# A two-layer decoder trunk on one core: FFN activations transposed by VectorE and a pass through DRAM, and a start by single k tiles over two DMA queues

## The chip, the cores and the metric

The kernel runs on one core of a Trainium2 chip. The metric is device time in microseconds from one launch. Three runs of the kernel before gave 1171.79, 1172.56 and 1173.34 us; the median is 1172.56 us.

The engines are called by their names in the profile: PE (TensorE, matrix products), PEld (its weight loads), DVE (VectorE), ACT (ScalarE), POOL (GpSimd), and SP (SyncE), which here only issues DMAs. SPq and ACTq are the DMA-issuing rows of SP and ACT.

## What is computed

A trunk of two layers over 256 tokens of width 1024. Each layer is a half-step SwiGLU FFN, a gated mix of three token mixers (a diagonal state-space model, sparse attention, forgetting attention), and another half-step FFN; a final RMSNorm follows. The change is in the four FFNs and in the start of the first one:

```python
def swiglu(h, w_gate, w_up, w_down):
    return (jax.nn.silu(h @ w_gate) * (h @ w_up)) @ w_down

x = x + 0.5 * swiglu(rms_norm(x, g), w_gate, w_up, w_down)   # hidden width 2816 = 22 k tiles of 128
```

## The kernel before, in words

**Split products.** Every weight is loaded as fp32 in a *unit* of two k tiles (256 rows) by up to 512 columns: `raw`, 512 KB, four buffers. ACT rounds it to fp32r (`hi<-raw`), DVE takes the rest (`lo<-raw,hi`). The tokens' side is split in the same way: `h0h`, `h0l` (k tiles 0 to 3 of the FFN's input), `h1h`, `h1l` (4 to 7), and `ath`, `atl` (the hidden activations). Each k tile and half of the tokens then takes three matmuls: high by high, high by low, low by high (`mm_tok`).

**An FFN.** `ffn` goes through the 2816 hidden columns in five chunks of 512 and one of 256. A chunk has four units of the gate weights and four of the up weights, so 96 matmuls into four PSUM banks (`ps_acc`). Halfway ACT computes `s` (SiLU of the gate part, line 662); at the end DVE computes `act = up * rstd * s` (line 670), with tokens on the partitions. The down product contracts over the hidden columns, so it needs `act` with hidden columns on the partitions. The generator `up_T` (lines 627 to 640) makes it: per pair of k tiles four PE transposes of 128x128 into a scratch PSUM bank `ps_t`, one ACT copy to `ath`, one DVE subtraction to `atl`. That is 176 transposes in 44 groups of four for the whole program. The down product (lines 677 to 683) then runs over 22 k tiles, twice (two halves of 512 output columns).

**What sets the order.** The program writes one instruction stream per engine in a fixed order; at run time each engine goes through its stream in order and waits on semaphores. While the stream is written, a `Clock` adds up estimated costs per engine. After each group of matmuls `tick` (line 325) lets background generators such as `up_T` go one step if their input should be ready by that clock, and `feed` issues the `hi` and `lo` work of the units ahead: up to four and three units ahead of PE. A unit's DMA is issued on SP when its buffer is free, that is behind the `lo` of the unit four before it (line 378). `prep_once`, `prep_bias` and `prep_layer` are background generators too; they compute constants of the mixers, most of them on DVE, beside the first FFN of each layer.

**The start.** `run` (line 1395) issues the column constants `cols`, then on the one queue SP in turn pieces of the transposed input `xT` (by 1, 1, 2 and 4 k tiles) and gate units; the first two units have one k tile each. `first_T` makes `h0h`/`h0l` of a k tile from `xT`. `loads` (line 1223) then brings the input `x` with tokens on the partitions, from which ACT computes the sums of squares for `rstd`; `s` of the first chunk waits for it.

Of the kernel before, what the change touches and what calls it, by code (L numbers as in the profile page):

```python
# [18 lines left out]
P = 128  # L19
# [33 lines left out]


# [23 lines left out]
def plan(a):  # L78
# [3 lines left out]
    def add(w, k0, nk, c0, n):  # L82
        k = k0
        while k < k0 + nk:
            m = min(2 if len(units) > 1 else 1, k0 + nk - k)
            units.append((w[k * P:(k + m) * P, c0:c0 + n].rearrange("(k p) c -> p k c", p=P), m, n))
            k += m

    def ffn(l, which):
        wg, wu, wd = (a[f"{which}_w_{n}"][l] for n in ("gate", "up", "down"))  # L90
        for i, (c0, n) in enumerate(f_chunks()):
            order = [(wg, 0), (wu, 0), (wg, 4), (wu, 4)] if i == 0 else [(wg, 0), (wg, 4), (wu, 0), (wu, 4)]
            for w, k0 in order:
                add(w, k0, 4, c0, n)
        for d in range(2):
            for k0 in range(0, FK, 4):
                add(wd, k0, min(4, FK - k0), d * 512, 512)
# [136 lines left out]
class Trunk:  # L234
# [112 lines left out]
    def feed_dma(self, upto):  # L347
        while self.n_dma < min(upto, len(self.units)):
            ap, nk, n = self.units[self.n_dma]
            t = self.rawp.tile([P, 2, 512], F32, tag="raw", name="raw")  # L350
            self.clock.after("dma", self.freed.get(self.n_dma - RAW_BUFS, 0.0))
            self.nc.sync.dma_start(t[:, :nk, :n], ap)
            self.raw[self.n_dma] = t
            self.n_dma += 1

    def feed_hi(self, upto):
        while self.n_hi < min(upto, len(self.units)):
            i = self.n_hi
            _, nk, n = self.units[i]
            self.feed_dma(i + 1)  # L360
            hi = self.piecep.tile([P, 2, 512], F32R, tag="hi", name="hi", bufs=HI_AHEAD + 1)
            self.nc.scalar.activation(hi[:, :nk, :n], self.raw[i][:, :nk, :n], AF.Copy)
            self.split_tiles[i] = hi
            self.n_hi += 1

    def feed_lo(self, upto):
        nc = self.nc
        while self.n_lo < min(upto, len(self.units)):
# [5 lines left out]
            nc.vector.tensor_tensor(lo[:, :nk, :n], src, hi[:, :nk, :n].bitcast(F32), op=OP.subtract)  # L374
# [25 lines left out]
    def mm_tok(self, ps, xs, k0, nk, n, first, last):  # L400

        mm = self.nc.tensor.matmul
        for k, hi, lo in self.weights(nk, n):
            k += k0
            xh, xl = xs(k)
            for t in range(2):
                c = slice(t * P, t * P + P)
                mm(ps[t][:, :n], xh[:, c], hi, start=k == first, stop=False)
# [207 lines left out]
    def ffn(self, nxt):  # L616
# [4 lines left out]
        with tc.tile_pool(name="ffn", bufs=1, side="left") as pool:  # L621
# [3 lines left out]
            pend = None  # L625

            def up_T(act, k0, nk):
                yield act
                for b in range(0, nk, 2):
                    i, ps = yield from self.bank()  # L630
                    for j in range(2):
                        for t in range(2):
                            nc.tensor.transpose(ps[:, j * T + t * P:j * T + t * P + P],
                                                act[:, t, (b + j) * P:(b + j + 1) * P], self.ident)
                    yield ps
                    h, lw = ath[:, k0 + b:k0 + b + 2], atl[:, k0 + b:k0 + b + 2]
                    p3 = ps.rearrange("p (k t) -> p k t", k=2)
                    nc.scalar.activation(h, p3, AF.Copy)
                    nc.vector.tensor_tensor(lw, p3, h.bitcast(F32), op=OP.subtract)
                    self.tfree(i)  # L640

            for ci, (c0, n) in enumerate(f_chunks()):
# [17 lines left out]
                act = pool.tile([P, 2, 512], F32, tag="act", name="act", bufs=2)  # L660
# [8 lines left out]
                for t in range(2):  # L669
                    nc.vector.scalar_tensor_tensor(act[:, t, :n], pu[t][:, :n], rstd[:, t:t + 1], s[:, t, :n],  # L670
                                                   op0=OP.mult, op1=OP.mult)
                if pend:
                    self.finish(pend)
                pend = self.spawn(up_T(act, c0 // P, n // P), -1)
            ax = lambda k: (ath[:, k], atl[:, k])
            gens = []
            for d in range(2):
                ps = self.acc()
                last = nxt is None and d == 1
                for k0 in range(0, FK - LAST if last else FK, 2):  # L680
                    if d == 0 and k0 + 2 > FK - 2:
                        self.finish(pend)
                    self.mm_tok(ps, ax, k0, 2, 512, 0, FK - 1)
# [557 lines left out]
    def prep_bias(self, pool, begun):  # L1241
# [20 lines left out]
        yield from self.units_on(6)  # L1262
# [118 lines left out]
    def first_T(self, xT, k):  # L1381

        hi, lo = (n[:, k % 4] for n in self.nexthT[k // 4])
        g = self.cols[:, C_FFN1 + k:C_FFN1 + k + 1]
# [10 lines left out]
    def run(self):  # L1395
# [8 lines left out]
        warm = cst.tile([P, 1], F32, name="warm")  # L1404
        nc.scalar.activation(warm, self.ones[:, 0:1], AF.Silu)
# [5 lines left out]
        for l in range(L):  # L1411
            with tc.tile_pool(name="prep", bufs=1, side="right") as pp:
                gens = []
                if l == 0:
                    xT = pp.tile([P, KT, T], F32, tag="xT", name="xT")
                    for k, n, w in ((0, 1, 1), (1, 1, 2), (2, 2, 4), (4, 4, 4)):
                        nc.sync.dma_start(xT[:, k:k + n], a["l_xT"][:, k:k + n])
                        self.feed_dma(w)
                    self.nexthT = [self.new_hT(ch) for ch in range(2)]
                    for k in range(KT):  # L1420
                        self.first_T(xT, k)
                        if k < 4:
                            self.feed_lo(min(k + 1, LO_AHEAD))
                    begun = lambda: self.n_used > 7
                    self.s_gens = [self.spawn(self.loads(self.ss, lambda: self.n_used > 3, begun), -1)]
# [81 lines left out]
```

## Time and profile before

| | |
|---|---|
| median of three runs | 1172.56 us |
| profiled execution, its own time | 1173.79 us |
| its span, first to last instruction | 1172.0 us |
| PE busy | 1157.6 us (99%) |
| PEld, DVE, ACT, POOL busy | 83%, 67%, 52%, 7% |
| DMA | 208.07 MB, mean 178 GB/s |

The profiled execution lasted 1.79 us longer than its span, and 1.23 us longer than the median. A group row reads: line, engine, operation, output<-inputs, shapes, count, then busy us and mean ns of one, then idle time of that engine just before and who ended it. Line 217 is the helper through which every engine instruction is recorded, so groups are told apart by their tiles. Matmuls overlap in the pipe: one of 512 columns is shown with 0.39 us, but the next starts 0.227 us after it. So the cost of a PE instruction is read from the starts of its neighbours.

### The profile page before, as it was taken

What the parts mean: (1) busy time and instruction counts of PE and PEld (TensorE: products, weight loads), DVE (VectorE), ACT (ScalarE), POOL (GpSimd) and SP (SyncE); (2) the same over time, 40 slices, a digit from 0 to 9 for tenths busy, and PEclk for the clock granted to TensorE, in tenths of its full rate; (3) what the DMA queues carried; (4) which work ended last, traced back from release to release, by engine and by line L of the source; (5) the groups of instructions that cost most, each with busy time, mean ns of one, the idle gap of its engine ahead of it and who ended that gap; (6) DMA issues with size and microseconds to landing.
All of it is one profiled execution on the core that took longest, in us unless ns stands there. A gap on an engine that the chain in (4) does not pass through costs nothing.

```text
span 1172.0 us, 16482 instructions
## 1 busy us (share of the span) xinstructions
PE 1157.6 (99%) x5990; PEld 973.8 (83%) x5990; DVE 784.0 (67%) x1380; ACT 608.2 (52%) x905; POOL 85.7 (7%) x135
## 2 busy tenths in 40 slices
PE   8999999999999999999999999999999999999997
PEld 6888888998787888888888888889987788888885
DVE  4876975798777665555578646558977776555554
ACT  5544454644765554444455545446548655444442
POOL 1000700000210700000000000000013000000000
PEclk9999999999999999999999999999999999999999
DMA  7656655466444666646566546544744456655661
GB/s 270 223 173 178 209 162 178 153 189 183 124 149 152 193 198 190 184 146 223 193 189 181 174 143 221 185 150 146 234 128 140 157 189 197 190 179 162 206 193 69
DMA packets 115554, 208.07 MB, mean 178 GB/s; under 512 B 7486, under 2 KB 27376, under 8 KB 115472
## 3 DMA queue, kind: packets, MB, share of 16 engines
q1 hardware_dynamic: 114000, 203.51, 55.5%
q0 software_dynamic: 1184, 3.11, 1.0%
q8 instruction: 47, 0.77, 0.3%
q10 hardware_dynamic: 288, 0.39, 0.1%
q14 instruction: 35, 0.29, 0.1%
HBM read 205.91 MB, written 1.07 MB: 177 GB/s over the span
## 4 chain that ended last, share of the span: by engine, by line
PE 96%; ACT 2%; DVE 1%; DMA 1%; issue 0%; SPq 0%; ACTq 0%; DVEq 0%
PE ps_acc L217 88%; PE ps_t L217 8%; DMA raw<-in_ffn_w_gate_dram 1%; ACT vT L217 1%; ACT hi L217 0%; ACT st L217 0%; DVE lo L217 0%; SPq L217 0%; DVE st L217 0%; ACT ahl L217 0%; DVE rsqt L217 0%; DVE bl L217 0%; DVE rstd L217 0%; ACT bh L217 0%; ACT junk L217 0%
## 5 line engine op out<-in xcount | busy, mean ns | idle before, releaser
L217 DVE TENSOR_TENSOR lo<-raw,hi 128x1024 fp32r<-128x1024 f32 (+3 forms) x415 | 468.5, 1136 | 228.7 <-PE ps_acc L217 190.2
L217 ACT ACTIVATE hi<-raw 128x1024 fp32r<-128x1024 f32 (+3 forms) x415 | 408.3, 989 | 356.2 <-PE ps_acc L217 278.2
L217 PE MATMUL ps_acc<-hi,h0h 128*128 128x512 f32 (+3 forms) x544 | 212.1, 390 | 2.7 <-ACT hi L217 2.6
L217 PE MATMUL ps_acc<-hi,h1h 128*128 128x512 f32 (+3 forms) x544 | 208.4, 383 | 0.0
L217 PE MATMUL ps_acc<-lo,h0h 128*128 128x512 f32 (+3 forms) x544 | 205.6, 378 | 1.0 <-DVE lo L217 1.0
L217 PE MATMUL ps_acc<-hi,h0l 128*128 128x512 f32 (+3 forms) x544 | 205.2, 377 | 0.0
L217 PE MATMUL ps_acc<-hi,h1l 128*128 128x512 f32 (+3 forms) x544 | 204.3, 376 | 0.0
L217 PE MATMUL ps_acc<-lo,h1h 128*128 128x512 f32 (+3 forms) x544 | 204.2, 375 | 0.0
L217 PE MATMUL ps_acc<-hi,ath 128*128 128x512 f32 x352 | 139.0, 395 | 0.0
L217 PE MATMUL ps_acc<-hi,atl 128*128 128x512 f32 x352 | 137.3, 390 | 0.0
L217 PE MATMUL ps_acc<-lo,ath 128*128 128x512 f32 x352 | 137.2, 390 | 0.0
L217 PEld LDWEIGHTS ps_acc<-hi,h0h 128*128 128x128 f32 x544 | 103.0, 189 | 20.9 <-ACT hi L217 3.9
L217 PEld LDWEIGHTS ps_acc<-lo,h0h 128*128 128x128 f32 x544 | 103.2, 190 | 18.4 <-DVE lo L217 2.3
L217 PEld LDWEIGHTS ps_acc<-hi,h1h 128*128 128x128 f32 x544 | 102.6, 189 | 19.1 <-issue 1.8
L217 PEld LDWEIGHTS ps_acc<-hi,h0l 128*128 128x128 f32 x544 | 103.0, 189 | 18.1
L217 PEld LDWEIGHTS ps_acc<-hi,h1l 128*128 128x128 f32 x544 | 102.5, 188 | 18.0
L217 PEld LDWEIGHTS ps_acc<-lo,h1h 128*128 128x128 f32 x544 | 102.6, 189 | 16.8 <-issue 0.2
L217 PEld LDWEIGHTS ps_acc<-hi,atl 128*128 128x128 f32 x352 | 66.1, 188 | 13.8
L217 PEld LDWEIGHTS ps_acc<-hi,ath 128*128 128x128 f32 x352 | 66.2, 188 | 13.5 <-issue 0.4
L217 PEld LDWEIGHTS ps_acc<-lo,ath 128*128 128x128 f32 x352 | 66.2, 188 | 13.3 <-issue 0.2
L217 DVE TENSOR_TENSOR atl<-ps_t,ath 128x512 fp32r<-128x512 f32 x44 | 30.4, 691 | 28.9 <-ACT ath L217 28.7
L217 ACT ACTIVATE ath<-ps_t 128x512 fp32r<-128x512 f32 x44 | 26.1, 594 | 32.4 <-PE ps_t L217 32.4
(270 smaller groups left out, 1227.8 us busy)
## 6 DMA issues: line engine op xcount, KB each, us to landing
raw<-in_ffn_w_down_dram SPq DMA_DIRECT2D x88, 512.0 KB, 4.3
raw<-in_ffn_w_up_dram SPq DMA_DIRECT2D x80, 512.0 KB, 4.1
raw<-in_ffn_w_gate_dram SPq DMA_DIRECT2D x79, 512.0 KB, 4.3
raw<-in_w_in_dram SPq DMA_DIRECT2D x56, 512.0 KB, 4.6
raw<-in_w_out_dram SPq DMA_DIRECT2D x16, 512.0 KB, 3.7
raw<-in_ffn_w_gate_dram SPq DMA_DIRECT2D x18, 256.0 KB, 2.8
raw<-in_ffn_w_up_dram SPq DMA_DIRECT2D x16, 256.0 KB, 2.8
raw<-in_w_in_dram SPq DMA_DIRECT2D x16, 256.0 KB, 2.8
```

The source lines that it names most:

```text
L217: return f(*args, **kw)
```

## The change

`up_T` no longer uses PE. DVE writes `act` with its columns reordered: hidden column 16i+m of a chunk goes to place 32m+i (in the chunk of 256: 8i+m), so successive results are written 128 bytes apart. DVE then transposes `act` by blocks of 32x32 within each group of 32 partitions (`STREAM_TRANSPOSE at<-act`, one instruction per half of the tokens). SP writes `at` to a scratch tensor in DRAM (`actd<-at`, 512 KB in 256 runs of 2 KB for a chunk of 512) and, once that has landed, reads it back (`aT<-actd`, 512 KB in 1024 runs of 512 bytes) so that hidden column 4p+k of the chunk stands on partition p. `ath` and `atl` are computed from `aT` in SBUF instead of from PSUM. The rows of `w_down` are loaded in the same order ("(p k) c"). `act` has one buffer instead of two, and the down product waits chunk by chunk (`ups`) while the stream is written.

At the start, `xT` is issued from ACT's queue ahead of its table load, and the gate units from SP's; the first two units have two k tiles each but are loaded and split by single k tiles, alternating with `first_T`; for these k tiles the two matmuls that need `lo` come last. `x` is called for earlier (`n_used > 1`), and the bias rows later (10 units instead of 6).

```diff
--- before.py
+++ after.py
@@ plan @@
-    def add(w, k0, nk, c0, n):
+    def add(w, k0, nk, c0, n, rows="(k p) c -> p k c"):
         k = k0
+        part = w[k0 * P:(k0 + nk) * P, c0:c0 + n].rearrange(rows, p=P)
         while k < k0 + nk:
-            m = min(2 if len(units) > 1 else 1, k0 + nk - k)
-            units.append((w[k * P:(k + m) * P, c0:c0 + n].rearrange("(k p) c -> p k c", p=P), m, n))
+            m = min(2, k0 + nk - k)
+            units.append((part[:, k - k0:k - k0 + m], m, n))
...
-                add(wd, k0, min(4, FK - k0), d * 512, 512)
+                add(wd, k0, min(4, FK - k0), d * 512, 512, "(p k) c -> p k c")
@@ feed_dma, feed_hi, feed_lo (SINGLE = 2) @@
-            self.nc.sync.dma_start(t[:, :nk, :n], ap)
+            for j in self.parts(self.n_dma):
+                self.nc.sync.dma_start(t[:, j, :n], ap[:, j])
...
+    def parts(self, i):
+        nk = self.units[i][1]
+        return [slice(j, j + 1) for j in range(nk)] if i < SINGLE else [slice(0, nk)]
...
-            self.nc.scalar.activation(hi[:, :nk, :n], self.raw[i][:, :nk, :n], AF.Copy)
+            if i >= SINGLE:
+                self.nc.scalar.activation(hi[:, :nk, :n], self.raw[i][:, :nk, :n], AF.Copy)
...
-            nc.vector.tensor_tensor(lo[:, :nk, :n], src, hi[:, :nk, :n].bitcast(F32), op=OP.subtract)
+            for j in self.parts(i):
+                if i < SINGLE:
+                    self.first_T(j.start + 2 * i)
+                    nc.scalar.activation(hi[:, j, :n], src[:, j], AF.Copy)
+                nc.vector.tensor_tensor(lo[:, j, :n], src[:, j], hi[:, j, :n].bitcast(F32), op=OP.subtract)
@@ mm_tok @@
+            early = self.n_used <= SINGLE
+            if early:
+                for t in range(2):
+                    c = slice(t * P, t * P + P)
+                    mm(ps[t][:, :n], xh[:, c], hi, start=k == first, stop=False)
+                    mm(ps[t][:, :n], xl[:, c], hi, start=False, stop=False)
             for t in range(2):
                 c = slice(t * P, t * P + P)
+                if early:
+                    mm(ps[t][:, :n], xh[:, c], lo, start=False, stop=k == last)
+                    continue
...
@@ ffn @@
-            pend = None
+            ups = []
 
             def up_T(act, k0, nk):
+                n, m = nk * P, nk * 32
                 yield act
+                at = pool.tile([P, 2, 512], F32, tag="at", name="at")
+                for t in range(2):
+                    nc.vector.transpose(at[:, t, :n], act[:, t, :n])
+                    yield
+                yield at
+                scr = self.dram.tile([2, P, 512], F32, name="actd")
+                nc.sync.dma_start(bass.AP(tensor=scr.tensor, offset=scr.offset, ap=[[n, P], [P * n, 2], [1, n]]), at[:, :, :n])
+                yield scr
+                aT = pool.tile([P, 8, P], F32, tag="aT", name="aT")
+                nc.sync.dma_start(aT[:, :, :m], bass.AP(tensor=scr.tensor, offset=scr.offset, ap=[[m, P], [32 * n, 8], [1, m]]))
+                yield aT
                 for b in range(0, nk, 2):
-                    i, ps = yield from self.bank()
-                    for j in range(2):
-                        for t in range(2):
-                            nc.tensor.transpose(ps[:, j * T + t * P:j * T + t * P + P],
-                                                act[:, t, (b + j) * P:(b + j + 1) * P], self.ident)
-                    yield ps
-                    h, lw = ath[:, k0 + b:k0 + b + 2], atl[:, k0 + b:k0 + b + 2]
-                    p3 = ps.rearrange("p (k t) -> p k t", k=2)
-                    nc.scalar.activation(h, p3, AF.Copy)
-                    nc.vector.tensor_tensor(lw, p3, h.bitcast(F32), op=OP.subtract)
-                    self.tfree(i)
+                    h, lw = (x[:, k0 + b:k0 + b + 2].rearrange("p k (a j) -> p k a j", a=8) for x in (ath, atl))
+                    a4 = aT[:, :, b * 32:b * 32 + HD].rearrange("p a (k j) -> p k a j", k=2)
+                    nc.scalar.activation(h, a4, AF.Copy)
+                    nc.vector.tensor_tensor(lw, a4, h.bitcast(F32), op=OP.subtract)
+                    yield
...
-                act = pool.tile([P, 2, 512], F32, tag="act", name="act", bufs=2)
+                act = pool.tile([P, 2, 512], F32, tag="act", name="act")
...
-                    nc.vector.scalar_tensor_tensor(act[:, t, :n], pu[t][:, :n], rstd[:, t:t + 1], s[:, t, :n],
-                                                   op0=OP.mult, op1=OP.mult)
-                if pend:
-                    self.finish(pend)
-                pend = self.spawn(up_T(act, c0 // P, n // P), -1)
+                    o, p, g = (x.rearrange(f"p {r} -> p i m", i=32) for x, r in
+                               ((act[:, t, :n], "(m i)"), (pu[t][:, :n], "(i m)"), (s[:, t, :n], "(i m)")))
+                    nc.vector.scalar_tensor_tensor(o, p, rstd[:, t:t + 1], g, op0=OP.mult, op1=OP.mult)
+                ups.append(self.spawn(up_T(act, c0 // P, n // P), -1))
...
-                    if d == 0 and k0 + 2 > FK - 2:
-                        self.finish(pend)
+                    if d == 0 and k0 % 4 == 0:
+                        self.finish(ups[k0 // 4])
@@ prep_bias @@
-        yield from self.units_on(6)
+        yield from self.units_on(10)
@@ run @@
-        warm = cst.tile([P, 1], F32, name="warm")
-        nc.scalar.activation(warm, self.ones[:, 0:1], AF.Silu)
...
-                    for k, n, w in ((0, 1, 1), (1, 1, 2), (2, 2, 4), (4, 4, 4)):
-                        nc.sync.dma_start(xT[:, k:k + n], a["l_xT"][:, k:k + n])
-                        self.feed_dma(w)
+                    for k, n in ((0, 1), (1, 1), (2, 2), (4, 4)):
+                        nc.scalar.dma_start(xT[:, k:k + n], a["l_xT"][:, k:k + n])
+                    warm = cst.tile([P, 1], F32, name="warm")
+                    nc.scalar.activation(warm, self.ones[:, 0:1], AF.Silu)
+                    self.feed_dma(RAW_BUFS)
                     self.nexthT = [self.new_hT(ch) for ch in range(2)]
-                    for k in range(KT):
-                        self.first_T(xT, k)
-                        if k < 4:
-                            self.feed_lo(min(k + 1, LO_AHEAD))
+                    self.xT = xT
+                    self.feed_lo(SINGLE)
+                    for k in range(4, KT):
+                        self.first_T(k)
...
-                    self.s_gens = [self.spawn(self.loads(self.ss, lambda: self.n_used > 3, begun), -1)]
+                    self.s_gens = [self.spawn(self.loads(self.ss, lambda: self.n_used > 1, begun), -1)]
```

SP, the very start of the program, before: pieces of `xT` and units of weights in turn.

```order
L217 DMA cols<-in_l_cols_dram 128x114
L217 DMA xT<-in_l_xT_dram 128x256
L217 DMA raw<-in_ffn_w_gate_dram 128x512
L217 DMA xT<-in_l_xT_dram 128x256
L217 DMA raw<-in_ffn_w_gate_dram 128x512
L217 DMA xT<-in_l_xT_dram 128x512
L217 DMA raw<-in_ffn_w_gate_dram 128x2x512
L217 DMA raw<-in_ffn_w_up_dram 128x2x512
L217 DMA xT<-in_l_xT_dram 128x1024
L217 DMA raw<-in_ffn_w_up_dram 128x2x512
```

The same place on SP now:

```order
L221 DMA cols<-in_l_cols_dram 128x114
L221 DMA raw<-in_ffn_w_gate_dram 128x512 x4
L221 DMA raw<-in_ffn_w_up_dram 128x2x512 x2
L221 DMA raw<-in_ffn_w_gate_dram 128x2x512 x2
L221 DMA raw<-in_ffn_w_up_dram 128x2x512 x2
L221 DMA x<-in_x_dram 128x1024 x2
```

The four pieces of `xT` have left SP; they are the first four rows of ACT's stream, ahead of its table load. Four single k tiles of gate weights stand directly behind `cols`.

DVE, a chunk of 512 hidden columns in the second FFN of layer 0, before: `act`, then `atl` one unit later.

```order
L217 TENSOR_TENSOR lo<-raw,hi 128x1024 x3
L217 SCALAR_TENSOR_TENSOR act<-ps_acc,rstd,s 128x512 x2
L217 TENSOR_TENSOR lo<-raw,hi 128x1024
L217 TENSOR_TENSOR atl<-ps_t,ath 128x512 x2
L217 TENSOR_TENSOR lo<-raw,hi 128x1024 x7
```

The same place on DVE now:

```order
L221 TENSOR_TENSOR lo<-raw,hi 128x1024 x3
L221 SCALAR_TENSOR_TENSOR act<-ps_acc,rstd,s 128x32x16 x2
L221 TENSOR_TENSOR lo<-raw,hi 128x1024
L221 STREAM_TRANSPOSE at<-act 128x512 x2
L221 TENSOR_TENSOR lo<-raw,hi 128x1024 x5
L221 TENSOR_TENSOR atl<-aT,ath 128x512 x2
L221 TENSOR_TENSOR lo<-raw,hi 128x1024 x2
```

Two instructions per chunk are new, and `atl` has moved back by five units.

SP, the end of the same FFN, before (from the last up units of 512 columns on):

```order
L217 DMA raw<-in_ffn_w_up_dram 128x2x512 x4
L217 DMA raw<-in_ffn_w_gate_dram 128x2x256 x4
L217 DMA raw<-in_ffn_w_up_dram 128x2x256 x4
L217 DMA raw<-in_ffn_w_down_dram 128x2x512 x22
L217 DMA raw<-in_ffn_w_gate_dram 128x2x512 x2
```

The same place now:

```order
L221 DMA raw<-in_ffn_w_gate_dram 128x2x256
L221 DMA actd<-at 128x2x512
L221 DMA raw<-in_ffn_w_gate_dram 128x2x256 x2
L221 DMA aT<-actd 128x8x128
L221 DMA raw<-in_ffn_w_gate_dram 128x2x256
L221 DMA raw<-in_ffn_w_up_dram 128x2x256 x4
L221 DMA raw<-in_ffn_w_down_dram 128x2x512 x2
L221 DMA actd<-at 128x2x512
L221 DMA raw<-in_ffn_w_down_dram 128x2x512 x4
L221 DMA aT<-actd 128x8x128
L221 DMA raw<-in_ffn_w_down_dram 128x2x512 x2
L221 DMA actd<-at 128x2x256
```

Each trip stands as a write, two to four units of weights, and a read, on the queue that loads the weights; the last read (`aT<-actd 128x8x64`) stands behind the tenth down unit of 22.

## Rows read from the trace of the kernel before

**Rows 1.** Page, part 1, busy time of each engine, and part 4, the chain.

```profile
PE 1157.6 (99%) x5990; PEld 973.8 (83%) x5990; DVE 784.0 (67%) x1380; ACT 608.2 (52%) x905; POOL 85.7 (7%) x135
...
PE 96%; ACT 2%; DVE 1%; DMA 1%; issue 0%; SPq 0%; ACTq 0%; DVEq 0%
```

**Rows 2.** Who waited for whom, PE: total us, times, longest.

```profile
PE ps_acc L217 <- ACT hi L217: 2.6, 1, 2.6
```

**Rows 3.** Groups by line and shape, PE: the transposes of act.

```profile
L217 PE MATMUL ps_t<-ident,act 128*128 128x128 f32 x176 | 26.6, 273 | 0.0
```

**Rows 4.** The chain in order of time: start us, us, what.

```profile
38.68 21.13 PE ps_acc L217 x93
59.82 0.44 PE ps_t L217 x4
```

**Rows 5.** Timeline of PE around one group: start us, us, instruction.

```profile
59.42 0.39 PE L217 MATMUL ps_acc<-hi,h0l 128*128 128x512 f32 x1
59.66 0.60 PE L217 MATMUL ps_t<-ident,act 128*128 128x128 f32 x4
60.01 0.47 PE L217 MATMUL ps_acc<-hi,h0h 128*128 128x512 f32 x1
60.32 0.39 PE L217 MATMUL ps_acc<-lo,h0h 128*128 128x512 f32 x1
```

**Rows 6.** Groups by line and shape, DVE.

```profile
L217 DVE TENSOR_TENSOR lo<-raw,hi 128x1024 fp32r<-128x1024 f32 x333 | 405.4, 1223 | 189.3 <-PE ps_acc L217 156.8 <-ACT hi L217 22.5 <-issue 8.1
...
L217 DVE TENSOR_TENSOR atl<-ps_t,ath 128x512 fp32r<-128x512 f32 x44 | 30.4, 691 | 28.9 <-ACT ath L217 28.7
...
L217 DVE TENSOR_TENSOR_SCAN w<-mg,w 128x256 f32<-128x256 f32 x8 | 5.1, 674 | 0.0
```

**Rows 7.** Instructions on the tile act, 40 to 110 us: ns min/median/max, starts.

```profile
L217 DVE SCALAR_TENSOR_TENSOR act<-ps_acc,rstd,s x6: 750/751/752, 56.5 to 102.5; 128x512 f32<-128x512 f32 x6
```

**Rows 8.** Stretches: us, busy (count) of PE, PEld, DVE, ACT, POOL, clock, DMA share, GB/s.

```profile
117.20:146.50 29.30, 29.30 (x175) 24.57 (x174) 26.57 (x42) 14.51 (x22) 21.76 (x42) 1.00 0.64 209
429.10:451.80 22.70, 22.70 (x105) 18.84 (x105) 12.46 (x13) 10.85 (x12) 0.00 (x0) 1.00 0.62 186
```

**Rows 9.** Timeline of SP's DMA issues in one chunk.

```profile
62.81 2.54 SPq L217 DMA_DIRECT2D raw<-in_ffn_w_gate_dram  x2
```

**Rows 10.** DMA queues (packets, MB, share), then issues (count, KB each, us to landing).

```profile
q1 hardware_dynamic: 114000, 203.51, 55.5%
...
raw<-in_ffn_w_up_dram SPq DMA_DIRECT2D x80, 512.0 KB, 4.1
...
raw<-in_ffn_w_up_dram SPq DMA_DIRECT2D x16, 256.0 KB, 2.8
...
out_dram<-y_t SPq DMA_DIRECT2D x2, 320.0 KB, 2.7
```

**Rows 11.** Timeline of the first 24 us: SP, ACT and PE.

```profile
3.53 0.43 SPq L217 DMA_DIRECT2D raw<-in_ffn_w_gate_dram  x1
...
3.85 0.51 ACT L217 ACTIVATE h0h<-xT,cols 128x256 fp32r<-128x256 f32 x1 [1.62 <-DMA xT<-in_l_xT_dram]
...
4.59 0.63 ACT L217 ACTIVATE hi<-raw 128x512 fp32r<-128x512 f32 x1 [0.23 <-DMA raw<-in_ffn_w_gate_dram]
...
11.40 1.06 ACT L217 ACTIVATE hi<-raw 128x1024 fp32r<-128x1024 f32 x1 [0.85 <-DMA raw<-in_ffn_w_gate_dram]
...
14.04 1.70 ACT L217 ACTIVATE h1h<-xT,cols 128x256 fp32r<-128x256 f32 x4 [1.18 <-DMA xT<-in_l_xT_dram]
...
23.34 0.39 PE L217 MATMUL ps_acc<-hi,h1h 128*128 128x512 f32 x1
```

**Rows 12.** The same view, stretches of the start.

```profile
5.30:10.00 4.70, 4.29 (x12) 2.38 (x12) 1.82 (x3) 1.15 (x2) 0.34 (x1) 1.00 0.91 315
10.00:12.50 2.50, 0.00 (x0) 0.00 (x0) 0.49 (x2) 1.60 (x3) 0.00 (x0) 1.00 1.03 402
12.50:17.00 4.50, 3.73 (x9) 2.80 (x10) 3.57 (x7) 3.32 (x7) 0.00 (x0) 0.62 0.70 232
```

More of the change, by code (lines that the diff above doesn't have):

```diff
@@ L52 @@
 WARM = 9
+SINGLE = 2
 RAW_BUFS = 4
@@ L1378, in prep_layer, with first_T @@
             yield
-    def first_T(self, xT, k):
+    def first_T(self, k):
         hi, lo = (n[:, k % 4] for n in self.nexthT[k // 4])
-        g = self.cols[:, C_FFN1 + k:C_FFN1 + k + 1]
+        g, xT = self.cols[:, C_FFN1 + k:C_FFN1 + k + 1], self.xT
         self.nc.scalar.activation(hi, xT[:, k], AF.Copy, scale=g)
```

## The prediction

> **What bounds the kernel now.** I read the page first: PE is busy 99% of the span and carries 96% of the chain that ended last [rows 1]. So only what shortens PE's stream, or the time in which it stands, can move the end. Then who waited for whom: the longest wait of PE on another engine is 2.6 us, once, for the first two-tile unit [rows 2]. The change touches both: it takes instructions out of PE's stream, and it rebuilds the start.
>
> **The transposes leave PE.** 176 of them stand in PE's stream [rows 3], in 44 groups of four. Their busy time (26.6 us) is not their price, since they overlap in the pipe. The price is read from starts: 93 matmuls of a chunk take 21.13 us, 0.227 each [rows 4]. Without the group, the matmul that starts at 60.32 would have started two steps after 59.42, at 59.87; it is 0.45 us late, of which 0.35 is the group and the rest the slower first matmul behind it [rows 5]. The chain gives the same 0.44 to a group [rows 4]. Gain: 44 x 0.445 = 19.6 us. Nothing takes their place on PE, and nothing else runs beside them, so all of it is on the path, if `ath`, `atl`, `hi` and `lo` still come in time.
>
> **What DVE gets.** 48 block transposes (40 of 512 columns, 8 of 256), and 48 `act` writes with a stride. The trace shows neither. For a transpose of 128x512 the nearest row is `atl`, same shape and type, 0.69 us; 512 columns more make `lo` 0.53 longer, which leaves out any fixed part, and the slowest rate, a scan of 256 columns in 0.67, makes it 1.35 [rows 6]. `act` costs 0.75 now [rows 7]; at the scan's rate 1.35. I take 0.69 and an unchanged 0.75, so +1.4 us a chunk (bounds +1.1 to +3.9). In the second FFN a chunk has 12.46 us of DVE work in 22.70 [rows 8]; with 1.4 more that is 13.9 in 21.8, and at the upper bound 16.4. The tight place is the end of the first FFN, where the mixers' constants are computed too: 26.57 busy of 29.30 [rows 8]. There three groups leave PE (28.0 stay) and the transposes of one long and the short chunk come, 1.4 + 0.8, giving 28.8. The 0.8 of excess lies within the one unit (2.7 us of PE) that `lo` is ahead, and the constants may slide into the down product. I price it at nothing; at the upper bounds (3.9 + 2.0) DVE would be 4.5 us behind. `atl` and `ath` keep their number and shape, and read SBUF instead of PSUM.
>
> [...]
>
> **The way through DRAM.** Each of 24 chunks adds a write and a read on SP's queue, 48 DMAs, and the read waits for the write. Behind the waiting read stand weight units, for which ACT's `hi` waits, and then PE. How much cover is there? The first gate unit of a chunk is issued at 62.81 [rows 9], and PE takes it when the chunk before ends, one period after the `act` at 56.5, at 79.2 [rows 4, 7]. Of these 16.4 us the landing takes about 4.1 [rows 10], `hi` 1.06 [rows 11] and `lo` 1.22 [rows 6]; 10 us are left. Two more units stand between write and read, 5.4 us of PE. So a write has to take over 15 us before PE sees it. A store of 320 KB to DRAM took 2.7 us, a load of 512 KB 4.1 [rows 10]. I expect 3 to 5 us for the write and 4 to 7 for the read, and no wait of PE. For the last chunk the read stands behind the tenth down unit and its tiles are needed with the eleventh; 16.4 us ahead are six units, so even there about 16 us remain.
>
> The 16 DMA engines are busy 62% of a chunk, 14.1 us [rows 8]. The write, 256 runs of 2 KB, is like a unit: at the queue's mean (55.5% of 16 x 1172 us over 114000 packets, 91 ns) 16 packets per engine, 1.5 us [rows 10]. The read has 64 packets of 512 bytes per engine: 5.8 us at 91 ns. But units with the same 256 packets at half the bytes land in 2.8 instead of 4.1 us [rows 10], so a packet costs largely by its bytes, and I take 41 ns, 2.6 us. Sum 18.2 of 21.8 us (21.4 at 91 ns). It fits either way.
>
> **The start.** Before, 48 matmuls lie between PE's first and the first that uses `h1h`, at 23.34 [rows 11]; at 0.227 they would need 10.9 us. [...] The two-tile gate unit, issued at 3.53, lands at 11.4; the second half of `xT` at 14.0 [rows 11]. The issue at 3.53 is SP's seventh, in steps of about 0.47; the fourth gate tile is now its fifth, at 2.6, 0.9 earlier, and `xT`'s second half, SP's ninth before, is ACT's fourth, 2.4 earlier. If landings move by as much, the tile is there at 10.5 and all of `xT` by 11.6. Then ACT does `h1h` (1.7, to 13.3), `hi` of the first up unit (1.06), DVE its `lo` (1.22, to 15.6), and 24 matmuls are left, 5.4: 21.0 instead of 23.34. Gain 2.3 us. Floor, if no transfer is late: ACT was ready at 2.2 (3.85 less its wait of 1.62 [rows 11]) and is so four issues of 0.43 later, at 3.9; it does four times 0.51 + 0.63 [rows 11], then the same chain: 17.9, a gain of 5.4. Other end: no earlier landing and, with waits at each tile, a lower clock for longer: 24.0, a loss of 0.7. I take 2.3, nearest to the row of the landing. `x` is asked for one unit earlier, so `s` should still free its banks in time.
>
> Sum for the profiled execution: 1173.79 - 19.6 - 2.3 = 1151.9; it lay 1.23 above the median of the runs, so 1150.7.
>
> **Rivals.**
> 1. The start gives nothing. For it: from 10.0 to 12.5 the DMA engines are at 100% of their share and 402 GB/s [rows 12], so two queues load the same engines, and `xT`'s last 512 KB now shares them with the gate tiles instead of standing behind. Against: from 5.3 to 10.0 only 315 GB/s moved. Price: T = 1150.7 + 2.3 + up to 0.7, about 1153.4. [...]
> 2. The start reaches its floor: 3.1 us more, 1147.6. It needs landings that the trace does not show.
> 3. DVE is late in the first FFN: the new operations run at the upper bounds, and PE waits for `lo` in the last chunks, 2 to 4.5 us: 1154.7, to 1155.2. If the third and fourth chunk are late too, 1157. For it: DVE is 91% busy there [rows 8]; against: the rows of two inputs at 0.69 to 0.75 for 512 columns. [...]
> 4. Slower than before: the DMA engines become the bound by the read in 512-byte runs. A chunk now takes 22.70; with 14.1 + 1.5 of other transfers it takes longer when 64 packets exceed 7.1 us, 112 ns each. At 120 ns it is 23.24, +0.54 on each of 20 long chunks and some 1 us on the short ones, less 2.3: 1182. Against: that is more than the mean of packets 3.5 times as large.
>
> **How the numbers follow.** Forecast 0.55, rival 1 0.17, rival 2 0.10, rival 3 0.11, rival 4 0.07, of which 0.02 end near its point of balance. The forecast's own range follows from the start's bounds, 1148 to 1154; with rivals 1 to 3 it becomes 1146.5 to 1157, which leaves out rival 4 and a little beyond. About 0.2% (2.3 us) is what a measurement of this kernel can tell from no change. Faster by more: all but rival 4, 0.93; within it 0.02; slower 0.05.
>
> **What would show it.** No `ps_t<-ident,act` on PE, and a chunk's chain of 96 matmuls in 21.8 us instead of 22.7; if chunks take longer, name who PE waits for: `lo` means rival 3, `hi` behind `raw` means rival 4. `STREAM_TRANSPOSE` near 0.7 us and `act` near 0.75. `actd` landing under 15 us. The first `h1h` matmul near 21.0, with the clock no lower than before. The prediction is wrong if PE's waits after the start exceed a few us in sum, or if the start ends later than 24.

## The result and the profile after

The changed kernel takes 1155.93 us (median of 4 runs, 1154.11 to 1158.91) beside 1172.95 of the kernel before in the same comparison: ratio 0.9854, 95% interval 0.9842 to 0.9866, so 17.1 us less (15.7 to 18.5). The forecast was 1150.7, 21.9 less. Of the expected gain 4.8 us are missing. The time lies in the stated range of 1146.5 to 1157, but not in the forecast's own part of it, 1148 to 1154. The profiled execution of the changed kernel is the slowest of its four (1158.91, 3.0 above the median), which has to be kept in mind wherever its microseconds are summed.

The page of the changed kernel, busy time of the engines and the chain that ended last:

```profile
PE 1139.4 (98%) x5814; PEld 956.4 (83%) x5814; DVE 819.0 (71%) x1427; ACT 606.5 (52%) x908; POOL 87.5 (8%) x135
...
PE 85%; DMA 6%; DVE 5%; ACT 2%; issue 1%; SPq 0%; DVEq 0%; ACTq 0%
```

PE has 176 instructions fewer, as many as there were transposes [rows 1, 3]. But PE's share of the chain fell from 96 to 85%, and DMA and DVE stand there with 11: the end now hangs on something else in places. The groups that belong to the four FFNs' activations, over the whole program (busy us, mean ns of one, idle before), DVE's and then ACT's:

```profile
L221 DVE SCALAR_TENSOR_TENSOR act<-ps_acc,rstd,s 128x512 f32<-128x512 f32 x40 | 43.1, 1164 | 9.4 <-PE ps_acc L221 9.4
...
L221 DVE TENSOR_TENSOR atl<-aT,ath 128x512 fp32r<-128x512 f32 x44 | 29.0, 697 | 62.0 <-ACT ath L221 62.0
L221 DVE STREAM_TRANSPOSE at<-act 128x512 f32<-128x512 f32 x40 | 25.7, 682 | 0.0
```
```profile
L221 ACT ACTIVATE ath<-aT 128x512 fp32r<-128x512 f32 x44 | 25.6, 625 | 47.7 <-DMA aT<-actd 47.7
```

The transpose costs 682 ns (0.69 us was taken). `act` went from 751 ns [rows 7] to 1164. And DVE stands 62.0 us ahead of `atl`, where it stood 28.9 before [rows 6]: the wait for the trip through DRAM is inside DVE's line, by way of ACT. The landings (issues, KB each, median us from issue to landing; the down weights took 4.3 before):

```profile
raw<-in_ffn_w_down_dram SPq DMA_DIRECT2D x88, 512.0 KB, 5.2
...
actd<-at SPq DMA_DIRECT2D x20, 512.0 KB, 5.8
aT<-actd SPq DMA_DIRECT2D x20, 512.0 KB, 5.5
```

The start: timeline of ACT and PE, then the view by windows, whose stretches answer to [rows 12].

```profile
10.92 1.70 ACT L221 ACTIVATE h1h<-xT,cols 128x256 fp32r<-128x256 f32 x4
...
20.20 0.39 PE L221 MATMUL ps_acc<-hi,h1h 128*128 128x512 f32 x1
```
```profile
5.30:10.00 4.70, 3.68 (x10) 2.93 (x11) 2.30 (x5) 2.85 (x6) 0.34 (x1) 1.00 1.03 391
10.00:12.50 2.50, 2.50 (x13) 2.06 (x12) 2.41 (x6) 2.36 (x6) 0.00 (x0) 1.00 1.04 374
12.50:17.00 4.50, 3.62 (x15) 2.48 (x14) 4.23 (x6) 3.69 (x5) 0.00 (x0) 1.00 0.68 194
```

`h1h` begins 3.1 us earlier and without a wait. PE works from 10.0 to 12.5, where it stood, and the granted clock stays at its upper level after that (1.00 from 10.0 to 24.0). The 1.00 of the first stretch has to be read with care: the record of the granted clock begins at 9.4, and the matmuls from 6.9 to 8.2 start 0.43 us apart, the pace that the kernel before shows from 14.4 to 16.5 at the lower level, a granted clock of 0.50. The first `h1h` matmul is at 20.20 instead of 23.34 [rows 11], and a chunk of the second FFN takes 21.76 us on PE instead of 22.69.

**Where the gain is lost.** PE runs the same 5088 accumulating matmuls (those into `ps_acc`) in both kernels, from the 25th on in the same order, so the same one can be looked up in both traces. The 801st stands in the second half of the first layer's first down product, behind all 11 groups of that FFN; before, then after, in the timeline of PE:

```profile
196.23 0.39 PE L217 MATMUL ps_acc<-hi,atl 128*128 128x512 f32 x1
```
```profile
194.21 0.39 PE L221 MATMUL ps_acc<-hi,atl 128*128 128x512 f32 x1
```

It is 2.0 us earlier. It should be 3.1 (start) and 11 groups by 0.445 (4.9) earlier, 8.0. So 6.0 us are lost by then. At the 3301st (761.11, and 751.42) 8.1 are lost, at the last matmul 7.9: the rest of the program keeps its gain, but for 2.1 us in the second layer's first FFN, which e7 (below), with the same order on every engine, does not show. The place is that first down product, up to the turn from its first half to its second. Its stretches after (us, busy of PE, PEld, DVE, ACT, POOL, clock, DMA share, GB/s), and one of the kernel before:

```profile
125.00:141.00 16.00, 16.00 (x94) 14.20 (x93) 10.19 (x15) 8.52 (x13) 9.07 (x26) 1.00 1.01 336
141.00:155.00 14.00, 14.00 (x58) 10.45 (x56) 13.43 (x16) 7.70 (x9) 13.61 (x15) 1.00 0.64 207
155.00:171.00 16.00, 12.38 (x56) 9.26 (x55) 14.98 (x19) 5.53 (x10) 1.55 (x2) 0.96 0.55 170
```
```profile
146.00:170.00 24.00, 24.00 (x142) 19.64 (x141) 16.20 (x25) 12.67 (x20) 1.14 (x2) 1.00 0.43 144
```

Before, DVE has 7.8 us of air in 24, once the constants are done. After, it first stands for 5.8 of 16 us, most of it in the 4.13 us ahead of one `atl`, and then works 28.4 of 30 while PE stands for 3.6. Its timeline shows why (start us, us; idle before and its cause in brackets), and PE's what came of it:

```profile
135.96 1.23 DVE L221 TENSOR_TENSOR lo<-raw,hi 128x1024 fp32r<-128x1024 f32 x1 [0.38 <-PE ps_acc L221]
141.32 1.39 DVE L221 TENSOR_TENSOR atl<-aT,ath 128x512 fp32r<-128x512 f32 x2 [4.13 <-ACT ath L221]
...
167.01 0.69 DVE L221 TENSOR_TENSOR bp<-pm,pm 64x512 f32<-64x512 f32 x1
167.73 1.22 DVE L221 TENSOR_TENSOR lo<-raw,hi 128x1024 fp32r<-128x1024 f32 x1
168.87 1.28 DVE L221 SCALAR_TENSOR_TENSOR x<-ps_acc,x 128x512 f32<-128x512 f32 x2
```
```profile
166.93 0.39 PE L221 MATMUL ps_acc<-hi,atl 128*128 128x512 f32 x1
169.61 0.33 PE L221 MATMUL ps_t<-ident,x 128*128 128x128 f32 x1 [2.29 <-DVE x L221]
```
```profile
169.60:173.40 3.80, 3.52 (x13) 2.89 (x13) 2.33 (x4) 3.21 (x8) 0.00 (x0) 0.55 0.60 190
```

The last line is a stretch of the view by windows. Who PE waited for between 20 and 190 us (total, times, longest):

```profile
PE ps_t L221 <- DVE x L221: 2.6, 2, 2.3
PE ps_acc L221 <- DVE lo L221: 0.9, 1, 0.9
```

`x`, which PE transposes for the next norm, stands behind DVE's backlog: `bp`, the last piece of the mixers' constants, and a `lo` come right ahead of it. PE waits 0.9 for a `lo` and 2.6 for `x`, and after the long wait the granted clock is 0.55 for 3.8 us, and 0.50 from 169.9 to 173.2, where matmuls of 512 columns start 0.43 us apart instead of 0.23; that costs an estimated 0.45 x 3.8 = 1.7. The sum is 5.2 of the 6.0; the rest is not assigned. PE's own order has a part in it too: the transposes of `x` stand behind the 714th accumulating matmul, where they stood behind the 717th, and three matmuls are 0.7 us.

### The profile page after: what moved, and what is told of

Read it like the earlier page. It is cut to its first block, busy times and chain, and to the rows that moved or that the text cites. A ratio compares the mean times of both kernels' runs of the same rounds, so it can differ in the third digit from the quotient of the medians.

```text
span 1157.1 us, 16231 instructions
## 1 busy us (share of the span) xinstructions
PE 1139.4 (98%) x5814; PEld 956.4 (83%) x5814; DVE 819.0 (71%) x1427; ACT 606.5 (52%) x908; POOL 87.5 (8%) x135
## 4 chain that ended last, share of the span: by engine, by line
PE 85%; DMA 6%; DVE 5%; ACT 2%; issue 1%; SPq 0%; DVEq 0%; ACTq 0%
PE ps_acc L221 79%; PE ps_t L221 6%; DVE lo L221 2%; DMA aT<-actd 2%; DMA actd<-at 2%; DMA raw<-in_ffn_w_down_dram 1%; ACT hi L221 1%; DMA raw<-in_ffn_w_gate_dram 1%; DVE pm L221 0%; DVE atl L221 0%; DVE act L221 0%; DVE vT L221 0%; DMA raw<-in_ffn_w_up_dram 0%; ACT vT L221 0%; DMA xT<-in_l_xT_dram 0%
## 5 line engine op out<-in xcount | busy, mean ns | idle before, releaser
L221 ACT ACTIVATE hi<-raw 128x1024 fp32r<-128x1024 f32 (+4 forms) x416 | 407.2, 986 | 344.6 <-PE ps_acc L221 205.3
L221 DVE TENSOR_TENSOR lo<-raw,hi 128x1024 fp32r<-128x1024 f32 (+4 forms) x416 | 465.6, 1132 | 159.4 <-PE ps_acc L221 89.8
L221 PE MATMUL ps_acc<-hi,h0h 128*128 128x512 f32 (+3 forms) x544 | 207.8, 382 | 1.2 <-ACT hi L221 1.1
L221 PEld LDWEIGHTS ps_acc<-hi,h0h 128*128 128x128 f32 x544 | 102.9, 189 | 19.9 <-ACT hi L221 1.9
L221 DVE TENSOR_TENSOR atl<-aT,ath 128x512 fp32r<-128x512 f32 x44 | 29.0, 697 | 62.0 <-ACT ath L221 62.0
L221 DVE SCALAR_TENSOR_TENSOR act<-ps_acc,rstd,s 128x512 f32<-128x512 f32 (+1 forms) x48 | 47.9, 1084 | 9.4 <-PE ps_acc L221 9.4
```

The lines of the kernel that those rows point to most:

```text
L221: return f(*args, **kw)
```

## The experiments

Two explanations stood at first, and a third came up on the way: (A) DVE simply has too much to do, `act` above all; (B) the trip through DRAM holds it up, either because `atl` and `ath` stand too early in line for the real landing (B1) or because the traffic slows the weights (B2); (C, later D) the planner, the `Clock` that fixes the order, put the constants' work off, so that it ends right ahead of `x`. Gains below are (1 - ratio) x 1173 us, each from a comparison with the kernel before on the same chip. "Lost" is worked out as above, on the profiled execution (its own time stands in the column before), with that execution's own start.

| kernel | median us | ratio, 95% interval | gain | profiled run | lost at the 801st | PE waits for x |
|---|---|---|---|---|---|---|
| changed | 1155.93 | 0.9854 [0.9842, 0.9866] | 17.1 | 1158.91 | 6.0 | 2.6 |
| e1 start only | 1170.16 | 0.9971 [0.996, 0.9981] | 3.4 | 1170.08 | 0 | none |
| e2 trip only | 1158.93 | 0.9876 [0.9859, 0.9893] | 14.5 | 1161.45 | 7.9 | 2.6 |
| e3 act contiguous | 1153.74 | 0.9836 [0.9821, 0.985] | 19.2 | 1152.19 | 2.3 | 2.0 |
| e4 no trip | 1150.49 | 0.9802 [0.9789, 0.9816] | 23.2 | 1151.57 | 1.3 | 1.0 |
| e5 landing in order | 1151.55 | 0.9825 [0.9812, 0.9839] | 20.5 | 1154.53 | 4.7 | 2.9 |
| e6 landing and act | 1163.21 | 0.9916 [0.9901, 0.9931] | 9.9 | 1162.35 | 12.0 | 6.7 |
| e7 strided reads | 1156.24 | 0.986 [0.9847, 0.9874] | 16.4 | 1156.93 | 7.4 | 2.6 |
| e8 bias at six | 1155.98 | 0.9859 [0.9846, 0.9872] | 16.5 | 1155.00 | 4.5 | 0.5 |
| e9 constants early | 1153.03 | 0.9829 [0.9816, 0.9843] | 20.1 | 1151.24 | 1.2 | none |
| e10 early, landing | 1151.62 | 0.9816 [0.9803, 0.9829] | 21.6 | 1151.62 | 1.0 | none |
| e11 from PSUM | 1153.23 | 0.983 [0.9816, 0.9843] | 19.9 | 1152.80 | 2.8 | 2.4 |
| e12 all three | 1152.30 | 0.9822 [0.9809, 0.9836] | 20.9 | 1152.28 | 2.2 | none |

**e1, the start alone**, on the kernel before:

```diff
+for k, n in ((0, 1), (1, 1), (2, 2), (4, 4)):
+    nc.scalar.dma_start(xT[:, k:k + n], a["l_xT"][:, k:k + n])
+self.feed_dma(RAW_BUFS)
...
+for j in self.parts(self.n_dma):
+    self.nc.sync.dma_start(t[:, j, :n], ap[:, j])
```

> The kernel before with only the new beginning: x's transpose from ScalarE's queue, the first two weight pairs by single k tiles, the first matmuls ordered hi before lo. Both theories of the missing 5 us put them behind the beginning, so both expect what the changed kernel's beginning shows: first h1h matmul at 20.2 us instead of 23.34, 3.1 us less, 1169.8 us (1168.8 to 1170.8). If the beginning works only as far as the prediction had it (21.0), it is 2.3 us, 1170.6; if nothing of it is kept to the end, 1172.9.

3.4 us (2.2 to 4.7), kept to the end.

**e2, the trip alone**: the changed kernel with the old beginning (the same lines, taken out).

> The changed kernel with the old beginning, so only the transposes by VectorE and the way through DRAM. If the two parts add up, the change's 17.0 us less the beginning's 3.1 are 13.9, 1159.0 us (1158 to 1160). 44 groups by 0.445 us would be 19.6 and 1153.4: that would mean that the loss comes from the beginning's new order. Theory A (VectorE has too much to do at the ends of the first FFNs) and theory B (the trip's landing and its traffic hold the line there) both expect 1159.

14.5 (12.6 to 16.5). The parts add up within their intervals (3.4 + 14.5 against 17.1), and the loss is in the trip's part.

**e3, act written contiguously** (the output is another one):

```diff
-((act[:, t, :n], "(m i)"), (pu[t][:, :n], "(i m)"), ...
+((act[:, t, :n], "(i m)"), (pu[t][:, :n], "(i m)"), ...
```

> The changed kernel with act written in the order in which it is read, at neighbouring addresses; the reordering of columns is left out, so the output is another one. Order of instructions is the same. All theories: act 1.16 us falls to about 0.75 (44 of them, 18 us of VectorE's time). Theory A: VectorE's excess at the ends of the first FFNs is part of the missing 5 us, four chunks there by 0.83 us are 3.3 us in the first layer and about 1 in the second: 1151.5 to 1153.5 us. Theory B: VectorE only waits there for the trip's landing: 1155 to 1156.5.

`act` falls to 746 ns, and 2 us come back, between the two theories; the intervals of this and the changed kernel just overlap. Some 18 us less work on DVE bring back no more than that, so most of the strided write is paid where it holds nobody up.

**e4, no trip:**

```diff
-at = pool.tile([P, 2, 512], F32, tag="at", name="at")
+at = pool.tile([P, 2, 512], F32, tag="at", name="at", bufs=2)
...
-nc.sync.dma_start(bass.AP(tensor=scr.tensor, ...), at[:, :, :n])
+self.clock.put("dma", 2 * P * n * 4 / 360e3, [scr], [at])
-nc.sync.dma_start(aT[:, :, :m], bass.AP(tensor=scr.tensor, ...))
+self.clock.put("dma", 2 * P * n * 4 / 360e3, [aT], [scr])
-a4 = aT[...]
+a4 = at[...]
```

> The changed kernel with ath and atl read straight from the transposed tile at: the write to DRAM and the read back are left out, so the exchange between groups of partitions is not done and the output is another one. VectorE's, ScalarE's and TensorE's instructions are the same in the same order. Theory B: without 11 us (in one chunk 16) of landing and without 22 MB of traffic the missing 5 us come back, 1150 to 1152. Theory A: VectorE's work is unchanged, 1154 to 1156.

All of the missing time comes back: 23.2, which is 19.6 + 3.4 and a rest of 0.2. The order is not quite the same, as had been expected: PE's is, but DVE has another instruction in 58 of 1427 places, and `at` has two buffers. DVE stands for 2.3 of the 16 us from 125 to 141 instead of 5.8, and PE for 1.0 us instead of 3.6 from 155 to 171, without the lower clock:

```profile
125.00:141.00 16.00, 16.00 (x95) 14.22 (x94) 13.71 (x21) 9.20 (x14) 9.05 (x21) 1.00 0.91 285
...
155.00:171.00 16.00, 15.03 (x73) 12.00 (x72) 14.35 (x20) 7.76 (x13) 2.65 (x3) 1.00 0.59 170
```

**e5, the landing as it is, in the planner:**

```diff
-done = start + cost + (1.8 if eng == "dma" else 0)
+done = start + cost + (1.8 if eng == "dma" else 0) + (2.3 if x.tensor.name.startswith(("actd", "aT")) else 0)
```

> The changed kernel, where the order is planned with 2.3 us more for the landing of each of the trip's two transfers (5.6 us for 512 KB instead of 3.3; 5.8 and 5.5 were measured). Same instructions, same traffic; ath and atl stand later in ScalarE's and VectorE's lines. Theory B1 (VectorE and ScalarE stop at atl and ath because these stand too early in line, 5.8 us of VectorE between 125 and 141 us): most of the 5.9 us that came back without the trip come back here, 1151 to 1153.5. Theory B2 (the trip's traffic slows the weights): nothing changes, 1155.5 to 1157.

1151.55: B1 as expected, and B2 is out as the main cause, since the traffic is all there. e7 and e8, compared in the same rounds, stayed at 1156. The profile caught the slowest of its four runs (1154.53), so its 4.7 us lost do not describe the median; how a run at the median looks is not known.

**e6, act's cost too:**

```diff
+if out.tensor.name.startswith("act_"): return 0.155 + n * 1.97e-3
```

> As the one with the landing in the planned order, and act planned at 1.16 us instead of 0.75. Theory B1 alone: as that one, within 0.7 us. Theory A (VectorE's excess is what the planner doesn't see): 1 to 2 us less than that one. B2: 1155.5 to 1157.

All three theories were wrong: 11.7 us slower than e5, with a planner that knows `act`'s cost better. One of its five executions took 5361 us, which nothing on record explains; the ratio leaves it out, and the median of the other four is 1162.92. PE's wait, and the stretches:

```profile
PE ps_t L222 <- DVE x L222: 6.7, 1, 6.7
```
```profile
141.00:155.00 14.00, 14.00 (x64) 11.58 (x63) 7.21 (x11) 7.06 (x12) 8.90 (x27) 1.00 0.82 256
155.00:171.00 16.00, 9.42 (x38) 6.44 (x36) 15.81 (x17) 3.75 (x4) 14.40 (x15) 1.00 0.45 133
171.00:185.00 14.00, 11.91 (x47) 9.65 (x48) 9.13 (x13) 7.41 (x13) 0.00 (x0) 0.76 0.46 142
```

DVE stands for half of 141 to 155 and is full right after. This led to theory D. Counted in `lo` on DVE (64 stand ahead of `x`, 63 in the kernel before), the constants' middle step (`sr`) and their last `bp` stand behind number 36 and 55 before, 42 and 63 in the changed kernel, 43 and 64 here. Behind the last `lo` but one ahead of `x` no constants' work stood before, one instruction (0.7 us) stands in the changed kernel, and four stand here (4.0 us; three of them take 1.1 instead of 0.69, in a stretch in which POOL is busy for 14.4 of 16 us). The fuller DVE looks to the planner, the longer it puts the constants off, until they are in front of `x`.

**e7, the reordering on the side of the reads:**

```diff
-o, p, g = (x.rearrange(f"p {r} -> p i m", i=32) ...
+o, p, g = (x.rearrange(f"p {r} -> p m i", i=32) ...
```

> The changed kernel with the reordering of act on the side of the reads: act is written at neighbouring addresses, the accumulator and s are read at steps of 64 bytes. Same order, same result. If only a strided write is slow, act takes 0.75 us and the time is that of the contiguous act, 1153 to 1154.5. If the two strided reads cost as much as the strided write (1.16), nothing changes, 1155.5 to 1157; if each costs it (1.6), 1157 to 1160.

`act` takes 1097 ns: no gain, as in its second case.

**e8, the bias earlier:** `units_on(10)` to `units_on(6)`.

> The changed kernel with the bias matmuls and their additions allowed from 6 weight units on, as before, instead of 10. Only the order around 110 to 160 us changes. Theory C (work put off to the end of the first FFN is what collides there): 2 to 4 us less, 1152.5 to 1154.5. Theory B1, which has VectorE stand still before that work: less than 1 us either way, 1155.5 to 1157.5.

No change in the time, but another loss in the place of the first. The last `bp` stands behind number 64; yet PE's wait for `x` is only 0.5 us. PE stood earlier, for the bias, and the granted clock was at its lower level from 141.0 to 144.4, right behind that (0.94 on average from 141 to 171; 1.00 from 125 to 141 and from 155 to 185):

```profile
PE ps_t L221 <- DMA toe<-reld: 1.9, 1, 1.9
```

`toe` is the table of the bias, 768 KB that POOL issues as part of the constants.

**e9, the constants early:**

```diff
-TICK, BACKLOG, PREP, EAGER = 1.5, 8.0, 0.0, -0.2
+TICK, BACKLOG, PREP, EAGER = 1.5, 8.0, 4, -0.2
```

> The changed kernel with 4.0 us instead of 0.0 of backlog that the planner allows for the constants' work. That puts it back to where it stood before the change, counted in weight units: sr's last step behind lo number 36 (before 36, changed 42), the last bp behind 56 (before 55, changed 63 of the 64 that stand ahead of x). The trip and act are as changed. Theory D (the planner, which counts VectorE fuller by the transposes, has put the constants off until they end right ahead of x, and TensorE waits for x): x's wait of 2.6 us and the half clock behind it go, 4 to 6 us less than changed, 1150.5 to 1152.5. Theory B1 alone (the trip's landing stops VectorE): the stop of 5.8 us stays, 1154.5 to 1157. Theory A alone (VectorE has too much work wherever it stands): TensorE waits for lo earlier instead, 1155 to 1158.

3.0 us more gain than the changed kernel; the intervals touch. PE's wait for `x` is gone and the lower clock with it:

```profile
125.00:141.00 16.00, 15.35 (x86) 12.45 (x85) 15.95 (x19) 7.04 (x8) 12.84 (x14) 1.00 0.73 228
...
155.00:171.00 16.00, 16.00 (x77) 13.28 (x75) 11.95 (x23) 8.86 (x15) 0.00 (x0) 1.00 0.57 189
```

The four runs lie at 1151.2, 1151.7, 1154.4 and 1154.8, so something of 3 us is still there in half of them; the median is 0.5 above what D expected. And e9 does not part D from B1. DVE's stop of 5.8 us is gone from 125 to 141 as well, for the edit also moves `toe`: its transfer is issued at 114.6, where the changed kernel issues it at 132.0, 0.9 us behind the read that took 9.5 us to land. Here that read takes 7.0. How much of that long landing was `toe`'s doing no run shows; without the trip (e4), with `toe` at 132.1, no more than 1.3 us are lost.

**e10, both:** the edits of e5 and e9.

> The constants early and the trip's landing in the planned order (5.6 us), together. Theory D with B1 as a smaller part: 1149.5 to 1151.5, at the level of the kernel without the trip (1150.5). B1 alone: as with the landing alone, 1151 to 1152.5. A: 1154 or more.

1151.62, five runs within 1 us: the largest gain of the versions that compute everything, 4.5 us more than the changed kernel's, with separate intervals; those of e5, e9, e11 and e12 overlap with it. It misses D's figure by 0.1. The 1.6 us between it and e4, whose intervals overlap, are an estimate of what the trip's traffic still costs.

**e11, the reordering from the accumulators:** e7's edit, and

```diff
-activation(s[:, t, :n], pg[t][:, :n], AF.Silu, ...)
+activation(s[:, t, :n].rearrange("p (m i) -> p m i", i=32), pg[t][:, :n].rearrange("p (i m) -> p m i", i=32), AF.Silu, ...)
```

> The changed kernel with the reordering of act's columns taken where the accumulators are read: ScalarE reads pg in steps of 64 bytes and writes s in the new order, VectorE reads pu in steps of 64 bytes; s is read and act written at neighbouring addresses. Same order, same result. If a strided read of an accumulator is free, act takes 0.75 us and s as before, and the time is the contiguous act's, 1153 to 1154.5. If it costs what the strided write does, act 1.1 us and s by 0.4 longer, 1155.5 to 1157.5.

```profile
L221 DVE SCALAR_TENSOR_TENSOR act<-ps_acc,rstd,s 128x512 f32<-128x512 f32 x40 | 28.3, 746 | 10.6 <-PE ps_acc L221 10.6
```
```profile
L221 ACT ACTIVATE s<-ps_acc,rstd 128x512 f32<-128x512 f32 x40 | 26.9, 688 | 14.4 <-PE ps_acc L221 14.3
```

`act` is back at 746 ns and `s` stays at 688 (689 in the changed kernel): reading an accumulator at steps of 64 bytes costs nothing here on either engine, and the time is that of e3.

**e12, all three:** the edits of e5, e9 and e11.

> The constants early, the trip's landing in the planned order, and the reordering taken from the accumulators, together: the three that each took time off, with the full result. If the loss of 6 us behind the first layer's first FFN was one thing with three ways out of it (room on VectorE ahead of x), they don't add up: what is left to gain is bounded by the forecast's own sum with the measured beginning, 19.6 + 3.4 us below before, 1149.9, so 1149 to 1151. If the strided write's 18 us of VectorE's time cost something elsewhere too, it is below that, 1147 to 1149.

1152.30, 1.3 us outside the expectation and no better than e10. The three ways don't add up, which fits one loss with three ways out of it.

## Why the prediction was right and where it was not

The time lies in the range, but above the forecast's own 1154. It lies there by the share that the rivals added, and near the price of rival 3, whose mechanism was the smaller part of the loss: so far it is luck. By the prediction's own sign (PE's waits after the start exceed a few us in sum) its account of the waits was wrong: from 20 us on they are 6.5 us, where the kernel before has 1.4.

- **The transposes leave PE, 19.6 us.** Right: a chunk takes 21.76 us (21.8 expected), and e4, which leaves out the trip alone, gains 23.2 (21.6 to 24.8), 19.6 and the start.
- **The start, 2.3 us (21.0).** Right in its steps, too small: 3.1 in the trace, 3.4 in e1. All of `xT` was there by 10.92 instead of the 11.6 expected, and PE's granted clock was 1.00 from 10.0 to 24.0, where the kernel before has 0.62 from 12.5 to 17.0 [rows 12]. No run shows the 0.7 us that the other end of the start (24.0) put on a lower clock for longer. Rival 1 is out, and the floor of rival 2 (17.9) was not reached. The 16 engines now run at 1.03 of their share from 5.3 to 10.0 us, where they had 0.91 [rows 12], so they had room for transfers issued earlier. How much of the 3 us that is stays open: e1 does not part the second queue from the single tiles and the new order of the first matmuls.
- **What DVE gets.** The transpose was right to 1%. `act` at an unchanged 0.75 was wrong: 1.16, inside the bounds, so a chunk brings 2.2 us instead of 1.4. The strides cost 0.41 us for a write of 512 elements at steps of 128 bytes (1164 ns, against 751 before), and 0.35 for a read at steps of 64 (1097 ns in e7, against 746 in e3).
- **"I price it at nothing": the step that failed.** It held that 0.8 us of excess at the end of the first FFN would be covered, and that the constants might slide into the down product. They did slide, all the way to `x`; the loss is 6.0 us in the profiled execution, and in the median 19.6 + 3.4 - 17.1 = 5.9. I summed DVE's work over a window, as if its order were free. The order is fixed by a planner that defers the constants whenever DVE looks full, so the new work on DVE moved them later (42 and 63 of 64), and `x` was the first work behind them on which PE waits at once: 2.6 us, with 1.7 for the clock behind it. e9 and e6 show it from both sides, though each moves other work too: earlier 3.0 us more gain, later 7.2 less.
- **"No wait of PE" for the trip.** Right for PE's tiles: cover of 15 us against 5.8 + 5.5, at worst 9.5 for one read. But only PE was asked. `ath` and `atl` stand in the lines of ACT and DVE, in front of `hi`, `lo` and the constants, placed for a landing of 3.3 us. The landing of 9.5 stopped DVE for 4.1 us at one `atl`, just where its work was needed next (the constants' `toe` moved beside it, as told under e9); without the trip (e4), or with the landing in the order (e5), the loss is smaller.
- **Rival 3** came nearest: DVE late at the end of the first FFN, 1154.7 to 1157 (by its own 2 to 4.5 us the lower end would be 1152.7). Its mechanism, PE waiting for `lo` in the last chunks by the sheer work, was the smaller part: taking the 0.41 us away (e3, e11) gave 2 to 3 us, putting the constants and the landing right (e10) 4.5.
- **Rival 4** did not happen: in the second FFN's stretch of the changed kernel PE is busy throughout, DMA at 0.77 of its share:

```profile
429.00:451.00 22.00, 22.00 (x99) 18.22 (x98) 14.25 (x15) 10.99 (x13) 0.00 (x0) 1.00 0.77 241
```

Open: why executions of one order differ by 3 to 5 us (changed 1154.1 to 1158.9; e9 in two groups). The landing of a 512 KB read spreads from 4.1 to 9.5 us, which would fit, but no run holds it fixed. In e9 the two slower executions have a mean granted clock of 0.996 and the two faster ones 0.998; those of the changed kernel do not sort that way.

## What to carry to other kernels

When a change adds work or a wait to an engine that is "only" three quarters busy, don't sum a window: list what stands behind the new instruction in that engine's line up to the first result on which the bound engine waits at once, and see whether that distance has shrunk. Where a planner sets the order, every cost added moves deferred work, and a truer cost can make things worse (e6) as long as the rule that defers doesn't know the deadline. Where a row has to be reordered, do it where an accumulator is read anyway (e11: 746 ns, against 1164 with the strided write).

## What the runs showed of the hardware

- 512 fp32 elements per partition on VectorE, one operand from an accumulator: 746 to 751 ns when SBUF is touched at neighbouring addresses; 1164 with the write at steps of 128 bytes, 1097 with the SBUF read at steps of 64 (e7), 746 with only the accumulator read at steps of 64 (e11). For reads of an accumulator at steps of 64 bytes by VectorE and ScalarE the rows show no cost (ScalarE's `s`: 688 in e11, 689 in the changed kernel).
- A block transpose (32x32 blocks) of 128x512 fp32 on VectorE takes 682 ns, of 128x256 420, as much as a two-input operation of the same size (`atl` 697, `w<-t,t` 422).
- Moving 512 KB out to DRAM took 5.8 us and back 5.5 at the median; the longest read took 9.5, in a stretch in which the DMA engines were at 1.01 of their share and the 768 KB of `toe` were under way too.
